# A dispatch kernel's weights as long rows dealt out by TensorE, and a third load cut in two with the stores held behind it

## The chip, the cores and the metric

The kernel runs on one core of one Trainium2 chip. The metric is device time in microseconds (us) of one execution; times given are medians of several runs. A core has five engines that run their own instruction streams (TensorE = PE, VectorE = DVE, ScalarE = ACT, GpSimd = POOL, SyncE = SP) and 16 DMA engines that move data between the main memory and the on-chip buffer of 128 partitions. In this program DMAs are issued from two queues: SyncE's, which the profile calls q1, and ScalarE's, which it calls q10.

## What is computed

Each token's row of 512 numbers is written out twice, each time multiplied by a weight of its own. `x` is 16 x 1024 tokens of 512 floats (33.5 MB), the weights are two floats a token, the output is 67 MB.

```python
def reference(x, expert_indices, expert_weights):
    k = expert_indices.shape[-1]              # 2
    x_expanded = x[:, :, np.newaxis, :].repeat(k, axis=2)
    weights = expert_weights[..., np.newaxis]
    return (x_expanded * weights).astype(np.float32)
```

The indices are not used beyond their shape.

## The kernel before

The 16,384 tokens are cut in five tiles of 25 tokens per partition and a last one of 3 (`groups`, `LAST`, L32 to L34): partition p of a tile holds 25 tokens that follow each other in memory, so that a load has 128 rows of 51,200 bytes. Two buffers hold x (`x_pool`, L44), a small one the last three tokens (`z_tile`), and a single buffer `o_ring` (L48) holds the output of one tile, 25 x 1024 floats per partition. Each tile's output is made and stored in two halves, tokens 0 to 12 and 13 to 24 (`emit`, L137), and the halves of the next tile go to the same places, so a half can only be filled again when its store has landed.

`fill` (L131) divides a half between two engines: VectorE takes the first 8 tokens (9 in the first tile) in `tensor_tensor` instructions of up to four tokens (L116), ScalarE the others in one `mul` for each token and weight (L106). Both read the weights from `w_tile`, where partition p holds the two weights of each of its tokens.

The order of the work is the program's order on each engine. ScalarE issues the loads of x: first 9 tokens of the first tile, then its other 16 (`FIRST`, L35), then the second tile (L79). The third tile's load goes out when the first tile's products are done (L147), with a small copy into `z_tile` ahead of it (L76) that makes the z load wait, and the z load behind it (L87). The fourth and fifth loads follow the second and third tiles. SyncE first issues six loads of weights (L93): for each tile 128 rows of 200 bytes, for the last three tokens 128 rows of 24 bytes. Behind them on the same queue stand all stores (L141), each of which waits for the products of its half.

Of the kernel before, what the change touches and what calls it, by code (L numbers as in the profile page):

```python
# [1 line left out]

# [4 lines left out]


@with_exitstack
def kernel(  # L10
    ctx: ExitStack,
    tc: tile.TileContext,
    x: bass.AP,
    expert_indices: bass.AP,
    expert_weights: bass.AP,
    out: bass.AP,
):
    nc = tc.nc

    batch, seq, hidden = x.shape  # L20
    k = expert_weights.shape[-1]
    P = nc.NUM_PARTITIONS
    ntok = batch * seq
    assert ntok % P == 0
    A_TOTAL = ntok // P

    f32 = mybir.dt.float32
    row = k * hidden
    CH = 4


    groups = [25, 25, 25, 25, 25]  # L32
    TX = max(groups)
    LAST = 3  # L34
    FIRST = [9, 16]  # L35
    SHARES = [[9, 9], [8, 8]]
    assert sum(groups) + LAST == A_TOTAL

    xf = x.rearrange("b s h -> (b s) h")
    of = out.rearrange("b s k h -> (b s) (k h)")  # L40
    wf = expert_weights.rearrange("b s k -> (b s) k")

    w_pool = ctx.enter_context(tc.tile_pool(name="w_pool", bufs=1))
    x_pool = ctx.enter_context(tc.tile_pool(name="x_pool", bufs=2))  # L44
    o_pool = ctx.enter_context(tc.tile_pool(name="o_pool", bufs=1))

    w_tile = w_pool.tile([P, A_TOTAL * k], f32)
    o_ring = o_pool.tile([P, TX * row], f32)  # L48

    def rows(of_all, done, T):  # L50
        return of_all[done * P : (done + T) * P, :].rearrange(
            "(p a) n -> p (a n)", a=T
        )


    if LAST:
        z_pool = ctx.enter_context(tc.tile_pool(name="z_pool", bufs=1))
        z_tile = z_pool.tile([P, LAST * hidden], f32)

    tiles = []  # L60
    done = 0
    for n in groups:
        tiles.append((done, n))
        done += n

    loaded = []

    def load(i):
        if i >= len(tiles):
            return  # L70
        done, n = tiles[i]
        x_tile = x_pool.tile([P, TX * hidden], f32)
        src = rows(xf, done, n)
        steps = FIRST if i == 0 else [n]
        if i == 2 and LAST:
            nc.scalar.copy(out=z_tile[:, :1], in_=o_ring[:, TX * row - 1 :])  # L76
        for e, step in enumerate(steps):
            at = sum(steps[:e])
            nc.scalar.dma_start(  # L79
                out=x_tile[:, at * hidden : (at + step) * hidden],  # L80
                in_=src[:, at * hidden : (at + step) * hidden],
            )
            if i == 0 and e == 0:
                for g in range(len(tiles) + 1):
                    weights(g)
        if i == 2 and LAST:
            nc.scalar.dma_start(out=z_tile, in_=rows(xf, A_TOTAL - LAST, LAST))  # L87
        loaded.append(x_tile)


    def weights(e):
        at, n = tiles[e] if e < len(tiles) else (A_TOTAL - LAST, LAST)
        nc.sync.dma_start(  # L93
            out=w_tile[:, at * k : (at + n) * k], in_=rows(wf, at, n)
        )

    def product(engine, o_tile, t, x_in, c, m):

        o = t * row
        if engine is not None:  # L100
            for e in range(m * k):
                out_e = o_tile[:, o + e * hidden : o + (e + 1) * hidden]
                in_e = x_in[:, e // k * hidden : (e // k + 1) * hidden]
                w_e = w_tile[:, c + e : c + e + 1]
                if engine is nc.scalar or engine is nc.any and (c + e) % 3 == 2:
                    nc.scalar.mul(out=out_e, in_=in_e, mul=w_e)  # L106
                else:
                    nc.vector.tensor_scalar(
                        out=out_e,
                        in0=in_e,  # L110
                        scalar1=w_e,
                        scalar2=None,
                        op0=mybir.AluOpType.mult,
                    )
            return
        nc.vector.tensor_tensor(  # L116
            out=o_tile[:, o : o + m * row].rearrange(
                "p (t k h) -> p t k h", t=m, k=k
            ),
            in0=x_in[:, : m * hidden]  # L120
            .rearrange("p (t h) -> p t h", t=m)
            .unsqueeze(2)
            .to_broadcast([P, m, k, hidden]),
            in1=w_tile[:, c : c + m * k]
            .rearrange("p (t k) -> p t k", t=m)
            .unsqueeze(3)
            .to_broadcast([P, m, k, hidden]),
            op=mybir.AluOpType.mult,
        )

    def fill(o_tile, x_in, c, m, v):  # L131
        for t in range(0, v, CH):
            u = min(t + CH, v)
            product(None, o_tile, t, x_in[:, t * hidden : u * hidden], c + t * k, u - t)
        product(nc.scalar, o_tile, v, x_in[:, v * hidden :], c + v * k, m - v)

    def emit(src, dst, c, cuts, shares):  # L137
        for at, to, v in zip(cuts, cuts[1:], shares):
            o_tile = o_ring[:, at * row : to * row]
            fill(o_tile, src[:, at * hidden : to * hidden], c + at * k, to - at, v)  # L140
            nc.sync.dma_start(out=dst[:, at * row : to * row], in_=o_tile)  # L141

    for i in range(2):
        load(i)
    for i, (done, n) in enumerate(tiles):
        emit(loaded[i], rows(of, done, n), done * k, [0, 13, n], SHARES[min(i, 1)])
        load(i + 2)  # L147
    emit(
        z_tile,
        rows(of, A_TOTAL - LAST, LAST),  # L150
        (A_TOTAL - LAST) * k,
        [0, LAST],
        [LAST],
    )

# [1 line left out]
_INS = ['x', 'expert_indices', 'expert_weights']  # L157
_OUTS = [((16, 1024, 2, 512), 'float32')]


# [23 lines left out]
```

## Time and profile before

| | |
|---|---|
| median of 3 runs | 239.5 us (239.43 to 239.72) |
| the profiled execution's own time | 239.73 us |
| its span, first to last instruction | 238.0 us |
| VectorE, ScalarE, GpSimd busy | 93.2, 55.2, 0.2 us |
| read from and written to main memory | 33.69 and 67.11 MB |
| mean rate over the span | 424 GB/s |

The page cuts the span in 40 slices of about 6 us; a digit is the busy share of a slice in tenths. The line of the DMA engines gives the mean of all 16. The queue lines give packets, megabytes and the time that the packets took as a share of 16 engines over the window asked for. A packet is one row of a transfer, or the small write that reports its end. In lists of instructions the columns are start, duration, engine, line and tiles (or, in groups, busy time and mean of one in ns, then idle time before).

### The profile page before, as it was taken

The page shows a single profiled execution, that of the slowest core. Times are in us where ns is not written, and L with a number is a line of the kernel's source. Part 1 is how long each engine was busy: PE and PEld are TensorE (multiplying, and loading weights), DVE is VectorE, ACT ScalarE, POOL GpSimd, SP SyncE. Part 2 cuts the span into 40 slices and gives each one's busy share as a digit, 9 for nine tenths or more (in the row PEclk, how much of TensorE's full clock was granted, in tenths as well). Part 3 has the DMA queues.
Part 4 walks back from the last instruction along what each step waited for, and adds up shares of the span by engine and source line. Part 5 has one row for each costly group of instructions (what it writes and reads, how often), then busy time and mean ns, then how long its engine had stood idle before and what let it go on. Part 6 is the DMA issues. An engine that isn't in the chain of part 4 may idle for free.

```text
span 238.0 us, 214 instructions
## 1 busy us (share of the span) xinstructions
DVE 93.2 (39%) x23; ACT 55.2 (23%) x88; POOL 0.2 (0%) x4
## 2 busy tenths in 40 slices
DVE  0599800000059193086005902920085292861300
ACT  0008800000054170081005302700080280800000
POOL 0000000000000000000000000000000000000000
DMA  6999999999999999999999999999999999999996
GB/s 252 445 415 493 475 415 414 415 386 457 430 406 397 434 439 456 458 430 415 405 435 484 430 434 434 413 405 431 490 430 448 417 397 423 457 448 438 438 397 264
DMA packets 3457, 100.80 MB, mean 424 GB/s; under 512 B 1152, under 2 KB 1152, under 8 KB 1280
## 3 DMA queue, kind: packets, MB, share of 16 engines
q1 hardware_dynamic: 2448, 67.24, 65.5%
q10 hardware_dynamic: 1008, 33.55, 33.1%
q14 instruction: 1, 0.01, 0.0%
HBM read 33.69 MB, written 67.11 MB: 424 GB/s over the span
## 4 chain that ended last, share of the span: by engine, by line
DMA 69%; DVE 16%; issue 5%; ACT 3%; ACTq 0%; DVEq 0%; SPq 0%
DMA out_dram<-o_ring 62%; DVE o_ring L116 16%; DMA x_tile<-in_x_dram 7%; ACT o_ring L106 2%; ACT L106 1%; ACTq L79 0%; DVEq L116 0%; SPq L141 0%; ACTq L106 0%
## 5 line engine op out<-in xcount | busy, mean ns | idle before, releaser
L116 DVE TENSOR_TENSOR o_ring<-x_tile,w_tile 128x4096 f32<-128x4096 f32 (+1 forms) x22 | 89.8, 4130 | 122.4 <-DMA out_dram<-o_ring 102.8
L106 ACT ACTIVATE o_ring<-x_tile,w_tile 128x512 f32<-128x512 f32 x86 | 53.7, 708 | 134.4 <-DMA out_dram<-o_ring 134.4
L116 DVE TENSOR_TENSOR o_ring<-z_tile,w_tile 128x3072 f32<-128x3072 f32 x1 | 3.4, 3359 | 7.0 <-DMA out_dram<-o_ring 7.0
L106 ACT ACT_TABLE_LOAD x1 | 1.3, 1283 | 18.8 <-DMA x_tile<-in_x_dram 18.8
L76 ACT COPY z_tile<-o_ring 128x1 f32<-128x1 f32 x1 | 0.2, 191 | 0.0
L168 POOL MEMSET const-bfloat16-1.0<- 128x1 bf16 x1 | 0.1, 102 | 0.0
L168 POOL MEMSET const-uint8-127<- 128x1 uint8 x1 | 0.1, 102 | 0.0
L168 POOL MEMSET const-float32-1.0<- 128x1 f32 x1 | 0.1, 99 | 0.0
L168 POOL MEMSET const-float32-0.0<- 128x1 f32 x1 | 0.1, 98 | 0.2 <-issue 0.2
## 6 DMA issues: line engine op xcount, KB each, us to landing
out_dram<-o_ring SPq DMA_DIRECT2D x5, 6656.0 KB, 32.7
out_dram<-o_ring SPq DMA_DIRECT2D x5, 6144.0 KB, 36.4
x_tile<-in_x_dram ACTq DMA_DIRECT2D x4, 6400.0 KB, 29.7
x_tile<-in_x_dram ACTq DMA_DIRECT2D x1, 4096.0 KB, 17.6
x_tile<-in_x_dram ACTq DMA_DIRECT2D x1, 2304.0 KB, 8.1
out_dram<-o_ring SPq DMA_DIRECT2D x1, 1536.0 KB, 14.6
z_tile<-in_x_dram ACTq DMA_DIRECT2D x1, 768.0 KB, 10.5
w_tile<-in_expert_weights_dram SPq DMA_DIRECT2D x5, 25.0 KB, 24.7
```

What stands on the lines that cost most here:

```text
L76: nc.scalar.copy(out=z_tile[:, :1], in_=o_ring[:, TX * row - 1 :])
L106: nc.scalar.mul(out=out_e, in_=in_e, mul=w_e)
L116: nc.vector.tensor_tensor(out=o_tile[:, o : o + m * row].rearrange("p (t k h) -> p t k h", t=m, k=k), in0=x_in[:, : m * hidden] .rearrange ...
L168: nc = _bacc.Bacc("TRN2", target_bir_lowering=False, num_devices=1)
```

## The change

Two things are changed.

Weights. For each of the five tiles the weights come as 16 rows of 1600 bytes (8 partitions' worth in each) in four DMAs, to the tail of `o_ring`, which is not yet in use. There, `deal` brings them to their 128 partitions: a VectorE copy puts the rows in line, eight TensorE transposes for each part turn 16 rows at a time, a VectorE copy puts them in order, a transpose turns them back, and a VectorE copy writes `w_tile`. The parts are tile 0, tiles 1 and 2, and tiles 3 and 4. The transposes need an identity matrix, which GpSimd makes with a memset and an `affine_select`. The last three tokens' weights come as before.

Loads and stores. The third tile is loaded as 21 and 4 tokens. The first tile's two stores are no longer issued behind their halves, but after a chain of three small GpSimd copies: the first reads two values that the 21-token load has brought, the second reads one value of each half of `o_ring`, the third writes these back, so that the stores, which read them, have to wait for it.

The order on the engines of the built program: on VectorE the lining copies of all three parts, two ordered copies, the first part's dealt weights and the third ordered copy stand ahead of the first product, and the other two parts' dealt weights between the first three products. On GpSimd a library reload stands between the memset and the select. On ScalarE the load of 21 tokens stands ahead of the small copy into `z_tile`, the loads of 4 tokens and of z behind it; the 21 tokens wait for ScalarE's fourteen products and for five of VectorE's six.

```diff
-    FIRST = [9, 16]
-    SHARES = [[9, 9], [8, 8]]
+    STEPS = {0: [9, 16], 2: [21, 4]}
...
+    parts = [(0, 1), (1, 3), (3, G)]
+    room = o_ring[:, TX * row - 2 * G * Q * c - len(parts) * P - P :]
...
+    def weights(g, to):
+        nc.sync.dma_start(
+            out=room[:R, g * Q * c : to * Q * c].rearrange(
+                "r (g m) -> r g m", g=to - g
+            ),
+            in_=wf[g * TX * P : to * TX * P, :].rearrange(
+                "(g r m) n -> r g (m n)", g=to - g, r=R
+            ),
+        )
+
+    def deal():
+        nc.gpsimd.memset(eye, 1.0)
+        nc.gpsimd.affine_select(
+            out=eye,
+            in_=eye,
+            pattern=[[-1, P]],
+            compare_op=mybir.AluOpType.is_equal,
+            fill=0.0,
+            base=0,
+            channel_multiplier=1,
+        )
+        back = ps_pool.tile([P, G * c], f32)
+        for e, (g, to) in enumerate(parts):
+            m = (to - g) * c
+            mid = ps_pool.tile([m, P], f32, name=f"mid{e}")
+            flat = turned[:m, e * P : (e + 1) * P]
+            near = lined[:, g * Q * c : to * Q * c].rearrange("r (q m) -> r q m", q=Q)
+            nc.vector.tensor_copy(
+                out=near.rearrange("r q (g n) -> r g q n", g=to - g),
+                in_=raw[:, g:to],
+            )
+            for q in range(Q):
+                nc.tensor.transpose(
+                    mid[:, q * R : (q + 1) * R], near[:, q, :], eye[:R, :R]
+                )
+            nc.vector.tensor_copy(
+                out=flat.rearrange("p (r q) -> p q r", q=Q),
+                in_=mid.rearrange("p (q r) -> p q r", q=Q),
+            )
+            nc.tensor.transpose(back[:, g * c : to * c], flat, eye[:m, :m])
+            nc.vector.tensor_copy(
+                out=w_tile[:, g * c : to * c], in_=back[:, g * c : to * c]
+            )
...
+    load(0, 0)
+    weights(0, 1)
+    weights(1, 3)
+    weights(3, 4)
+    weights(4, 5)
...
+    deal()
+    load(0, 1)
+    load(1, 0)
     for i, (done, n) in enumerate(tiles):
...
+        for at, to in halves:
+            make(x_pair[i % 2], done * k, at, to, 9 if i == 0 else 8)
+            if i > 0:
+                store(dst, at, to)
+        if i == 0:
+            nc.scalar.copy(out=z_tile[:, :1], in_=o_ring[:, TX * row - 1 :])
+            load(2, 0)
+            load(2, 1)
+            nc.scalar.dma_start(out=z_tile, in_=rows(xf, A_TOTAL - LAST, LAST))
+
+            nc.gpsimd.tensor_copy(out=hold, in_=x_pair[0][:, :2])
+            held = o_ring[:, : 13 * row + 1 : 13 * row]
+            nc.gpsimd.tensor_copy(out=hold, in_=held)
+            nc.gpsimd.tensor_copy(out=held, in_=hold)
+            for at, to in halves:
+                store(dst, at, to)
+        elif i + 2 < G:
+            load(i + 2, 0)
```

More of the change, by code (lines that the diff above doesn't have):

```diff
@@ L53, in rows @@
         )
-    if LAST:
-        z_pool = ctx.enter_context(tc.tile_pool(name="z_pool", bufs=1))
-        z_tile = z_pool.tile([P, LAST * hidden], f32)
     tiles = []
@@ L64 @@
         done += n
[L66 to L81, printed above, removed]
-            )
[L83 to L88, printed above, removed]
@@ L91, in weights, with load @@
[L91 to L95, printed above, removed]
+    def load(i, e):
+        at = sum(STEPS.get(i, groups[i : i + 1])[:e])
+        to = at + STEPS.get(i, groups[i : i + 1])[e]
+        part = slice(at * hidden, to * hidden)
+        nc.scalar.dma_start(out=x_pair[i % 2][:, part], in_=rows(xf, *tiles[i])[:, part])
+    G = len(groups)
+    R = 16
@@ L135, in fill, with make, store @@
         product(nc.scalar, o_tile, v, x_in[:, v * hidden :], c + v * k, m - v)
[L137 to L144, printed above, removed]
-    for i, (done, n) in enumerate(tiles):
[L146 to L154, printed above, removed]
+    def make(src, c, at, to, v):
+        o_tile = o_ring[:, at * row : to * row]
+        fill(o_tile, src[:, at * hidden : to * hidden], c + at * k, to - at, v)
+    def store(dst, at, to):
+        nc.sync.dma_start(
+            out=dst[:, at * row : to * row], in_=o_ring[:, at * row : to * row]
+        )
+    load(0, 0)
[3 more added lines that the diff above has]
+    weights(4, 5)
+    nc.sync.dma_start(
+        out=w_tile[:, G * c :], in_=rows(wf, A_TOTAL - LAST, LAST)
+    )
+    deal()
+    load(0, 1)
+    load(1, 0)
+    for i, (done, n) in enumerate(tiles):
+        dst = rows(of, done, n)
+        halves = [(0, 13), (13, n)]
+        for at, to in halves:
[15 more added lines that the diff above has]
+            load(i + 2, 0)
+    make(z_tile, (A_TOTAL - LAST) * k, 0, LAST, LAST)
+    store(rows(of, A_TOTAL - LAST, LAST), 0, LAST)
 _INS = ['x', 'expert_indices', 'expert_weights']
```

14 lines of the change are left out of this document (13 added, 1 removed).

## The prediction, made before the change was run

> **What bounds the kernel now.** I read the page first: the busy shares, the packet line and the queues.
>
> ```profile
> span 238.0 us, 214 instructions
> DVE 93.2 (39%) x23; ACT 55.2 (23%) x88; POOL 0.2 (0%) x4
> DMA  6999999999999999999999999999999999999996
> DMA packets 3457, 100.80 MB, mean 424 GB/s; under 512 B 1152, under 2 KB 1152, under 8 KB 1280
> ...
> q1 hardware_dynamic: 2448, 67.24, 65.5%
> q10 hardware_dynamic: 1008, 33.55, 33.1%
> ```
>
> No compute engine is busy for even half of the span, while the DMA engines stand at nine tenths in every slice but the first and the last. The two queues, q1 (SyncE: weights and stores) and q10 (ScalarE: loads of x), together take 98.6% of 16 engines over the span. So the span is the time in which 16 DMA engines move 100.8 MB, and only three things can change it: cheaper packets, DMA engines that stall on a packet, or a moment in which both queues are empty.
>
> Next come the queue lines of three windows: 5 to 45 us (loads with weight rows among them), 47 to 53 us (the three-token z tile, the last weights, the first stores) and 55 to 90 us (stores alone).
>
> ```profile
> q10 hardware_dynamic: 481, 17.68, 102.3%
> q1 hardware_dynamic: 481, 0.08, 1.1%
> ```
> ```profile
> q10 hardware_dynamic: 160, 0.79, 42.2%
> q1 hardware_dynamic: 259, 1.03, 41.9%
> ```
> ```profile
> q1 hardware_dynamic: 333, 15.50, 102.3%
> ```
>
> A packet is counted in the window where it begins, so a share may pass 100%; bytes over packet time give the rate all the same. Stores: 15.50 MB in 1.023 x 35 us is 433 GB/s. Loads: 17.68 MB in 1.023 x 40 us is 432 GB/s. The z tile: 0.79 MB in 0.422 x 6 us = 2.53 us of all engines, where 433 GB/s would need 1.82 us; **0.71 us is lost** there. Weight rows: 481 in 0.011 x 640 engine-us, that is 14.6 ns each. They are cheap, but they come one by one between the long x rows, which the landing times show:
>
> ```profile
> out_dram<-o_ring SPq DMA_DIRECT2D x5, 6656.0 KB, 32.7
> ...
> w_tile<-in_expert_weights_dram SPq DMA_DIRECT2D x5, 25.0 KB, 24.7
> ```
> ```profile
> DMA to landing us min/median/max: 5.3/32.1/49.0
> ```
>
> The second line is of the six weight DMAs alone: the first 25 KB take 5.3 us, the slowest DMA 49 us. The first store stands behind them on its queue, as the chain of waits has it:
>
> ```profile
> 25.12 42.86 DMA out_dram<-o_ring
> ```
>
> It lands at 67.98 us, and its 6.82 MB need 15.7 us at 433 GB/s, so it began at about 52 us, though it was issued at 25.12. No byte is lost by that, because q10 is full until then.
>
> **The change part by part.**
>
> (a) *Weights as long rows.* Out go 5 x 128 rows of 200 bytes; the 128 rows of 24 bytes stay. At 14.6 ns, 640 rows are 9.3 engine-us, over 16 engines 0.58 us. In come 80 rows of 1600 bytes. At 433/16 = 27.1 bytes per ns a row is 59 ns, and 200 bytes in 14.6 ns leave 7 ns beside the 7.4 for bytes, so 66 ns, five to an engine: 0.33 us. **Gain 0.25 us**; were the rows' fixed part nothing or twice as much, 0.28 to 0.21.
>
> (b) *The z tile moves beside stores.* Its rows were slow while they ran with only tiny rows on the other queue. After the change the stores are released when the 21 tokens have landed, and z's 6 KB rows alternate with 52 KB store rows. Where loads and stores alternate now, nothing is lost: the window from 95 to 99 us, in which the fourth tile's load sets in between stores, has
>
> ```profile
> DMA packets 38, 1.77 MB, mean 442 GB/s; under 512 B 4, under 2 KB 4, under 8 KB 4
> ```
>
> So between nothing and 0.71 us comes back. I take 0.65, near that row. The four tokens (8 KB rows, 1.05 MB, 2.42 us at 433 GB/s) now run alone before z. If they stalled as z did (2.53/1.82 = 1.39) they would lose 0.94 us. They lie 50 KB apart like the long rows and have no weight rows among them, so I take nothing; the 0.94 stays for the range. Splitting adds 8 packets of 7 ns to each engine: 0.06 us. **Gain 0.59 us.**
>
> (c) *The deal, and what waits for it.* New on the path of the first tile: GpSimd makes an identity, VectorE copies, TensorE transposes 27 times, VectorE copies back, and only then come the products. Who waits is seen in the timeline and the forms:
>
> ```profile
> 0.73 3.11 SPq L93 DMA_DIRECT2D w_tile<-in_expert_weights_dram  x6
> 0.73 8.50 ACTq L79 DMA_DIRECT2D x_tile<-in_x_dram  x3
> 8.90 19.73 DVE L116 TENSOR_TENSOR o_ring<-x_tile,w_tile 128x4096 f32<-128x4096 f32 x6 [8.90 <-DMA x_tile<-in_x_dram]
> ...
> 20.08 8.69 ACT L106 ACTIVATE o_ring<-x_tile,w_tile 128x512 f32<-128x512 f32 x14
> 25.12 197.72 SPq L141 DMA_DIRECT2D out_dram<-o_ring  x11
> 28.80 0.19 ACT L76 COPY z_tile<-o_ring 128x1 f32<-128x1 f32 x1
> 28.86 0.35 ACTq L79 DMA_DIRECT2D x_tile<-in_x_dram  x1
> ```
> ```profile
> L116 DVE TENSOR_TENSOR o_ring<-x_tile,w_tile 128x1024 f32<-128x1024 f32 x2 | 2.4, 1216 | 0.0
> L106 ACT ACT_TABLE_LOAD x1 | 1.3, 1283 | 18.8 <-DMA x_tile<-in_x_dram 18.8
> ...
> L168 POOL MEMSET const-uint8-127<- 128x1 uint8 x1 | 0.1, 102 | 0.0
> ```
>
> VectorE works without a gap from 8.90 to 28.63 us; ScalarE ends at 28.77, and the third tile's load is issued at 28.86 into the buffer that both have read. How late may it be? The lead from an issue to its first packet is about 1 us: issued at 0.73, packets begin in the slice from 1.5 us, in the first ten microseconds cut in quarters:
>
> ```profile
> DMA  0000001995393988969919919839879399300993
> ```
>
> In front of the third load q10 holds the second tile. The sixteen tokens ahead of that land at 18.79 (ScalarE's table load waited for them), and its 6.55 MB take 15.2 us more: landed at 34.0. I take 1.2 us, an estimate near the lead, between the first engine's last row and the landing: q10 runs dry at about 32.8, and the third load must be issued by 31.8. In the built program its 21 tokens wait for VectorE's fifth product only, not the sixth of 1.2 us, and for ScalarE's fourteen. VectorE's fifth ended at 28.63 - 1.22 = 27.4, so VectorE may be 4.4 us late and ScalarE 3.0 for nothing.
>
> How late is it? The built program puts on VectorE, ahead of the first product, three lining copies, three copies of transposes and one of the dealt weights; two more stand between the products. No such copy is in the trace; per column the 1024-column product gives 1.2 ns, so 800 columns are 0.95 us and 100 to 128 columns 0.15. The last weights, issued fourth at about 2.2 us, land 5.3 us later if they do as the first did: 7.5. Then a copy (0.95), eight transposes (no row; between 0.1 us, the smallest instruction shown, and 0.7 us, an ACTIVATE, and I take 0.1: 0.8), three short copies (0.45) and handovers: the first product starts at about 10 us instead of 8.9, and two copies (0.3) come later. VectorE is 1.4 us late, under 4.4. **Cost nothing**; the queue in front of the third load hides it. At 0.7 us per transpose the 24 first ones alone would take 17 us, and the cover would be gone; from there each microsecond is one.
>
> The other input is the identity. The built program has a library reload on GpSimd between the memset and the select. Its time is in no row: the small end is 0.1 us (MEMSET), then 1.28 us (the table load of ScalarE), then 5.3 us for 25 KB that come through the same busy DMA engines at that moment, and at the far end 24.7 us. I take 5.3: ready at 0.73 + 0.1 + 5.3 + 0.2 = 6.3 us, before the last weights. [...]
>
> (d) *The hold.* SyncE's first store waits for three tiny GpSimd copies behind the 21 tokens; behind it in SyncE's order stand all other stores, and ScalarE's and VectorE's work on the second tile waits for those. The chain: landing, three copies with handovers (0.1 us each by the MEMSET row, I take 0.2), issue and lead 1.0 us: 1.7 us. Meanwhile q10 still has the four tokens and z, 2.4 + 1.8 = 4.2 us. **Cost nothing**; at 1 us a copy the chain is 4 us and still covered.
>
> From there to the end stores follow without a gap as now; the fourth and fifth loads and the last products keep their places. Head and tail (1.6 us before the first packet, about 1.2 after the last) stay.
>
> **Sum:** 0.25 + 0.59 = 0.84, and about 0.05 for completion packets and rows that no longer make turns; call it 0.9. Against the profiled execution's span: 238.0 - 0.9 = 237.1 us. That execution took 239.73 us, 0.23 over the median of 239.5; the forecast for the median is **238.6 us**.
>
> **The rivals.**
>
> *The identity or the transposes come late* (ends slower). The place is the third load's issue; the price is 1 us for each microsecond of idle queue; it decides once the first product starts after 13.0 us (8.9 + 4.4 less the two later copies), that is, the identity later than about 10 us, with 2.6 us of transposes and copies behind it, or a library load longer than 9 us. For it: a small transfer among long rows has taken far more than 9 us (24.7). Against: at the start the same 25 KB took 5.3, and 4.4 us of cover is a lot. With a library load of 12 us the first product starts at 0.73 + 0.1 + 12 + 0.2 + 2.6 = 15.6, and the queue stands empty for 2.6 us: 239.5 - 0.9 + 2.6 = 241.2 us; at 24.7 it would be 254.
>
> *Stalls only change their place.* The four tokens lose what z lost, up to 0.94 us, or z stays slow beside the stores. For it: 8 KB rows are nearer to z's 6 KB than to anything else shown. Then only (a) is left, or a little less than nothing: 239.3 us.
>
> *The hold is late.* If GpSimd needs 2 us for each copy, stores begin 2.8 us after q10 ran empty: 239.5 - 0.9 + 2.8 = 241.4. Against it: the 0.1 us MEMSET.
>
> *It doesn't do what it says*: weights already cost only 0.6 us, so all of (a) could shrink by longer row times (1600 bytes as slow as z's rows, 1.39 x 66 ns, five to an engine, give 0.46 us in place of 0.33). Then 238.7, inside the forecast.
>
> **How the numbers follow.** Forecast 0.55; identity or transposes late 0.23; stalls moved 0.12; hold late 0.06; other delays, such as one DMA engine loaded with code and so behind the rest, 0.04. A measurement of this kernel can tell about 0.2% (0.5 us) from no change. The forecast's own range is 238.2 to 239.0, faster. Stalls moved is the same time. The other three are slower but for a few cases that miss the cover by under 1 us. That gives faster 0.55, same 0.14, slower 0.31. For 8 in 10 the range goes from 238.1 (all 0.58 us of weight rows and all 0.71 of z's) to 241.6, which takes in both late cases at their prices and leaves out only their far part.
>
> **What would show it.** Weights: q1 under 2% of the engines in the first ten microseconds and about 80 + 128 small rows in place of 768. Deal: first product at about 10 us, the 21 tokens' load issued at about 29 us, and no slice under nine tenths near 33 us. Hold: the first store issued near 47 us, no dip at 46 to 50 us. Stalls: z's rows near 433 GB/s over their packet time. The prediction is wrong if the DMA row dips near 33 or 48 us, if the first product starts after 13 us, or if rows of 8 KB show more than 0.3 us each.

## The result and the profile after

The changed kernel takes **243.4 us** (median of 6 runs, 243.06 to 244.9) against 239.61 us (239.43 to 239.81) for the kernel before on the same chip: ratio 1.0167 [1.0141, 1.0193], so 1.7% slower and well beyond the noise. The forecast was 238.6 us with a range of 238.1 to 241.6; the time lies outside it. The profiled execution, the longest of the six, took 244.9 us; its span of 243.2 us is 5.2 us longer than before's, where the medians differ by 3.8. Of the runs below, one execution of e13 was disturbed (245.55 us, against 241.5 to 241.68 of its other three) and is left out of that run's time and ratio; e13's trace, with the time of its third load, is of that execution.

The page of the changed kernel, the lines that answer to those of before:

```profile
span 243.2 us, 293 instructions
PE 3.4 (1%) x27; PEld 2.5 (1%) x27; DVE 95.9 (39%) x32; ACT 55.1 (23%) x88; POOL 1.3 (1%) x9
DMA  7999989999999999999999999999999999999992
DMA packets 3025, 100.80 MB, mean 415 GB/s; under 512 B 512, under 2 KB 592, under 8 KB 720
...
q1 hardware_dynamic: 1872, 67.24, 64.0%
q10 hardware_dynamic: 1152, 33.55, 33.5%
```

The change did what it says: 80 rows of 1600 bytes stand in place of 640 of 200, and the deal adds only 2.7 us to VectorE. The same bytes take longer, at 415 in place of 424 GB/s, and the page shows no hole, but for a dip to 8 in the sixth slice. Where the time went is in the order of events. The timeline of the changed kernel, its first 51 us (start, duration, engine; in brackets the idle time before and what ended it):

```profile
1.07 0.29 POOL L98 TENSOR_SCALAR_AFFINE_SELECT o_ring<-o_ring 128x128 f32<-128x128 f32 x1
3.08 0.36 DVE L113 COPY o_ring<-o_ring 16x400 f32<-16x400 f32 x1 [3.08 <-DMA o_ring<-in_expert_weights_dram]
...
8.44 0.56 DVE L113 COPY o_ring<-o_ring 16x800 f32<-16x800 f32 x1 [5.01 <-DMA o_ring<-in_expert_weights_dram]
...
12.19 0.56 DVE L113 COPY o_ring<-o_ring 16x800 f32<-16x800 f32 x1 [3.19 <-DMA o_ring<-in_expert_weights_dram]
...
14.32 4.41 DVE L149 TENSOR_TENSOR o_ring<-x,w_tile 128x4096 f32<-128x4096 f32 x1
...
33.28 0.33 ACTq L70 DMA_DIRECT2D x<-in_x_dram  x1
...
49.40 0.19 POOL L203 COPY hold<-x 128x2 f32<-128x2 f32 x1 [48.03 <-DMA x<-in_x_dram]
...
50.10 0.88 SPq L175 DMA_DIRECT2D out_dram<-o_ring  x2
```

The identity is ready at 1.36 us. The three lining copies wait for weights, the last until 12.19 us; so the first product starts at 14.32 us, the third load goes out at 33.28 us, its 21 tokens land at 49.40 us (the first GpSimd copy starts then) and the first store is issued at 50.10 us. The chain of waits shows what this becomes. First the changed kernel's stores in the chain (start, duration), then those of before behind its first one:

```profile
50.10 20.28 DMA out_dram<-o_ring
...
79.41 25.27 DMA out_dram<-o_ring
...
113.62 27.66 DMA out_dram<-o_ring
...
160.78 33.23 DMA out_dram<-o_ring
```
```profile
76.99 24.96 DMA out_dram<-o_ring
...
110.89 25.75 DMA out_dram<-o_ring
...
156.12 32.68 DMA out_dram<-o_ring
```

Start and duration give the landings: 70.38, 104.68, 141.28 and 194.01 us after, 67.98, 101.95, 136.64 and 188.80 before (the first from the chain row in the prediction). The kernel is 2.4 us late when the first of these stores has landed, 2.7 at the second, 4.6 at the third, 5.2 at the fourth. **About half of the loss of this execution is there when that store lands, at 70 us; most of the rest arises between 105 and 141 us.**

Part of the second half shows in the rows of the loads between 98 and 105 us, where the fourth load sets in (q10: packets, MB, share of 16 engines); the changed kernel first, then the one before:

```profile
q10 hardware_dynamic: 31, 1.59, 72.9%
```
```profile
q10 hardware_dynamic: 38, 1.95, 64.2%
```

1.59 MB in 0.729 x 7 us are 312 GB/s, before 434: 1.4 us of packet time that moves nothing. (The same kernel's second trace, e1, has only 0.3 us of it; see there.) And the end is frayed: the share of the DMA engines in the last slices of 2 us, after, then before.

```profile
236.00:238.00 2.00, 0.00 (x0) 0.00 (x0) 0.00 (x0) 0.00 (x0) 0.00 (x0) 1.00 0.98 418
238.00:240.00 2.00, 0.00 (x0) 0.00 (x0) 0.00 (x0) 0.00 (x0) 0.00 (x0) 1.00 0.32 135
240.00:242.00 2.00, 0.00 (x0) 0.00 (x0) 0.00 (x0) 0.00 (x0) 0.00 (x0) 1.00 0.09 37
```
```profile
236.00:238.00 2.00, 0.00 (x0) 0.00 (x0) 0.00 (x0) 1.00 0.08 31
```

After, some engines work on for more than 2 us while most are done (0.32 and 0.09); before, all stop within a microsecond (0.08 of 2 us). The packets of the trace say it more exactly. Of the 16 small writes that report the end of the last store, the last ones of the kernel, all end between 236.0 and 236.8 us before; after, 14 end between 238.3 and 239.5 us and two at 241.1 and 242.0. The kernel ends with its slowest engine.

### The profile page after: what moved, and what is told of

Same layout as the page of the kernel before. It is cut to its first block, busy times and chain, and to the rows that moved or that the text cites. A ratio compares the mean times of both kernels' runs of the same rounds, so it can differ in the third digit from the quotient of the medians.

```text
span 243.2 us, 293 instructions
## 1 busy us (share of the span) xinstructions
PE 3.4 (1%) x27; PEld 2.5 (1%) x27; DVE 95.9 (39%) x32; ACT 55.1 (23%) x88; POOL 1.3 (1%) x9
## 4 chain that ended last, share of the span: by engine, by line
DMA 53%; issue 24%; DVE 16%; POOL 0%; POOLq 0%; DVEq 0%; SPq 0%
DMA out_dram<-o_ring 53%; DVE o_ring L149 16%; POOL o_ring L98 0%; DVEq L149 0%; POOLq L237 0%; POOL o_ring L97 0%; POOL hold L203 0%; POOL hold L205 0%; SPq L175 0%; POOLq L205 0%; POOLq L226 0%
## 5 line engine op out<-in xcount | busy, mean ns | idle before, releaser
L149 DVE TENSOR_TENSOR o_ring<-x,w_tile 128x4096 f32<-128x4096 f32 (+1 forms) x22 | 89.9, 4128 | 112.9 <-DMA out_dram<-o_ring 102.2
L139 ACT ACTIVATE o_ring<-x,w_tile 128x512 f32<-128x512 f32 x86 | 53.7, 708 | 134.8 <-DMA out_dram<-o_ring 134.8
L113 DVE COPY o_ring<-o_ring 16x800 f32<-16x800 f32 (+1 forms) x3 | 1.5, 495 | 11.3 <-DMA o_ring<-in_expert_weights_dram 11.3
L118 PE MATMUL mid<-o_ring 16*100 16x16 f32 (+1 forms) x24 | 2.4, 230 | 11.4 <-DVE o_ring L113 11.4
L118 PEld LDWEIGHTS mid<-o_ring 16*100 16x100 f32 (+1 forms) x24 | 2.0, 169 | 11.7 <-DVE o_ring L113 8.1
L125 PE MATMUL back<-o_ring 100*128 100x100 f32 (+1 forms) x3 | 1.2, 401 | 4.5 <-DVE w_tile L126 4.5
L121 DVE COPY o_ring<-mid 100x128 f32<-100x128 f32 (+1 forms) x3 | 1.0, 387 | 0.2 <-PE mid L118 0.2
L126 DVE COPY w_tile<-back 128x100 f32<-128x100 f32 (+1 forms) x3 | 0.7, 236 | 0.3 <-PE back L125 0.3
L125 PEld LDWEIGHTS back<-o_ring 100*128 100x128 f32 (+1 forms) x3 | 0.5, 182 | 4.9 <-DVE w_tile L126 4.8
```

Of the source, the lines that this page charges most:

```text
L113: nc.vector.tensor_copy(out=near.rearrange("r q (g n) -> r g q n", g=to - g), in_=raw[:, g:to],)
L118: nc.tensor.transpose(mid[:, q * R : (q + 1) * R], near[:, q, :], eye[:R, :R])
L121: nc.vector.tensor_copy(out=flat.rearrange("p (r q) -> p q r", q=Q), in_=mid.rearrange("p (q r) -> p q r", q=Q),)
L125: nc.tensor.transpose(back[:, g * c : to * c], flat, eye[:m, :m])
L126: nc.vector.tensor_copy(out=w_tile[:, g * c : to * c], in_=back[:, g * c : to * c])
L149: nc.vector.tensor_tensor(out=o_tile[:, o : o + m * row].rearrange("p (t k h) -> p t k h", t=m, k=k), in0=x_in[:, : m * hidden] .rearrange ...
```

## The experiments

Four explanations stood against each other. **Late load:** the third load comes too late to follow the second without a gap, and the hold has taken away the stores that would fill it. **Hold:** holding the stores costs by itself. **Weights:** the long rows and the deal cost by themselves. **Shifted buffers:** the hold's flag tile of 8 bytes a partition, kept in 32, moves x, z and `o_ring` in the built program from 128 to 160 modulo 256 bytes. Ratios are to the kernel before on the same chip (239.62 to 239.72 us). Where a recorded expectation says "table", it means `z_tile`.

| run | what it is | us, median | ratio |
|---|---|---|---|
| e1_again | changed kernel once more | 244.5 | 1.0197 [1.017, 1.0224] |
| e2_weights_alone | long rows and deal, no hold, third tile in one | 239.63 | 0.9999 [0.999, 1.0009] |
| e3_hold_alone | 21 + 4 and hold, short weight rows | 240.94 | 1.0047 [1.0031, 1.0063] |
| e4_deal_later | changed, tiles 1 to 4 dealt later | 241.96 | 1.0105 [1.0074, 1.0137] |
| e5_no_hold | changed, without the hold | 239.64 | 1.0003 [0.9992, 1.0014] |
| e6_more_cover | changed, z loaded ahead of the third tile, that in 18 + 7 | 241.1 | 1.0057 [1.0043, 1.0072] |
| e7_z_later | before, z behind the fourth load | 239.65 | 1.0001 [0.9992, 1.001] |
| e8_aligned | changed, flag tile of 256 bytes | 242.87 | 1.0142 [1.0122, 1.0161] |
| e9_hold_aligned | e3, flag tile of 256 bytes | 240.5 | 1.003 [1.0019, 1.0041] |
| e10_cover_aligned | e6, flag tile of 256 bytes | 240.59 | 1.0038 [1.0026, 1.005] |
| e11_no_hold_shifted | e5 with an 8-byte tile | 239.89 | 1.0014 [0.9998, 1.0029] |
| e12_hold_late | e9, products 2 x 1.22 us later | 240.46 | 1.0037 [1.0023, 1.0051] |
| e13_hold_later | e9, 3 x 1.22 us later | 241.6 | 1.0079 [1.0062, 1.0096] |
| e14_late_no_hold | before, 2 x 1.22 us later | 239.95 | 1.0011 [1.0, 1.0022] |
| e15_hold_latest | e9, 5 x 1.22 us later | 242.94 | 1.015 [1.0123, 1.0178] |
| e16_latest_no_hold | before, 5 x 1.22 us later | 239.73 | 1.0007 [0.9997, 1.0016] |
| e17_rows_adjacent | before, with 16 long rows a tile besides, into adjacent partitions | 244.95 (one execution) | none |
| e18_rows_spread | e17, the rows into every eighth partition | 243.89 (one execution) | none |

### Each half alone

> The changed kernel once more, unedited, to see which of its losses come back. In the first profile the packet times beyond those of before sum to (per engine): 1.1 us up to 10 us (loads beside the weight rows), 1.0 us at 32 to 36 us (queue dry, the third load issued at 33.28), 1.4 us at 98 to 105 us (fourth load's first rows up to 4.1 us), and the slowest engine ends 2.5 us further behind the middle one than before. Theory A (late first product): the first two and the spread come back, the 1.4 us at 98 us does not, span 241.3 to 242.0. Rival B (the handover of loads and stores makes all of it): the 1.4 us at the fourth load comes back too, span about 243.

The loss is there again: 244.5 us, and its trace has a span of 242.4 us, between the two that were expected. The first four stores of its chain land 2.4, 1.9, 3.8 and 4.4 us later than before's, so here too 1.9 us arise between the second and the third. But from 98 to 105 us q10 moves 2.20 MB in 0.774 x 7 us, 406 GB/s: 0.3 us lost, not 1.4. So the slow rows at 98 us aren't what makes that part each time; what does is not shown.

> The weights part alone: 16 rows a tile and the deal, but the third tile loaded in one step and the first tile's stores issued behind their halves, as before. Theory A (long weight rows and the late first product): 241 to 243 us, the third load issued after 33 us; but the stores may fill the dry moment near 34 us, since nothing holds them, which would bring it down to 240 to 241. Rival B (hold and split are to blame): 239.3 to 239.9.

```diff
-    STEPS = {0: [9, 16], 2: [21, 4]}
+    STEPS = {0: [9, 16]}
...
-            if i > 0:
-                store(dst, at, to)
+            store(dst, at, to)
...
```

The three GpSimd copies and the flag tile go too, and the third tile is loaded in one. 239.63 us: the weights' half neither gains nor loses, though its first product starts at 14.25 us.

> The other part alone: third tile as 21 and 4 tokens and the hold, weights as 128 rows of 200 bytes straight to their place. Theory A: first product at 8.9 us, third load issued at 28.9, no dry queue; the stores stand behind the weight rows until about 50 us as before, so 239.3 to 240.0 us. Rival B: the engines spread at 47 to 55 us and the time is 241 to 243 us.

```diff
-    weights(0, 1)
...
+    for e in range(G):
+        nc.sync.dma_start(
+            out=w_tile[:, e * c : (e + 1) * c], in_=rows(wf, *tiles[e])
+        )
...
-    deal()
...
```

240.94 us, between the two that were expected: the hold's half costs 1.3 us, though the third load goes out at 27.70 us. The halves add up to 1.3 us and the whole costs 3.8: they act on each other.

> The changed kernel with the deal of tiles 1 to 4 moved behind the first half's products on VectorE (a tiny copy that reads the third product's output makes it wait), so that the first product waits for the first tile's weights alone. Theory A: first product at about 10 us (x lands then), third load issued before 32 us, no dry queue at 32 to 36 us; gain 1.0 us of dry time and most of the 2.5 us of spread: 240 to 241.5 us. Rival B: no gain, 243 to 244 us, though the queue is no longer dry.

```diff
...
+            if i == 0 and at == 0:
+                turn(list(enumerate(parts))[1:])
...
```

Here `turn` is the part of `deal` behind the identity, called for the first tile's part ahead of the loop and for the others at this place. The first product moved up to 10.50 us, but the deal of the other tiles then held up the second half, and the third load was still issued at 32.98 us, only 0.3 us earlier. 241.96 us, with a wide interval; as a test of the late load it is inconclusive.

> The changed kernel without the hold: the first tile's stores are issued behind their halves again; the weights' rows, the deal and the 21 and 4 tokens stay. Theory A2 (the deal makes the third load late, and only the hold, which leaves both queues without work, turns that into lost time and into engines out of step): the third load is issued after 33 us as in the changed kernel, but the stores run, no idle time at 32 to 37 us, 239.4 to 239.9 us. Rival B2 (the step of 21 and 4 tokens is at fault): 241 us or more.

```diff
-            if i > 0:
-                store(dst, at, to)
+            store(dst, at, to)
...
-            nc.gpsimd.tensor_copy(out=hold, in_=x_pair[0][:, :2])
-            held = o_ring[:, : 13 * row + 1 : 13 * row]
-            nc.gpsimd.tensor_copy(out=hold, in_=held)
-            nc.gpsimd.tensor_copy(out=held, in_=hold)
```

The queue rows of its timeline (SyncE's stores, ScalarE's third load):

```profile
26.22 8.45 SPq L174 DMA_DIRECT2D out_dram<-o_ring  x2
33.21 0.34 ACTq L69 DMA_DIRECT2D x<-in_x_dram  x1
```

The third load is as late as in the changed kernel (33.21 and 33.28 us), but stores stand in the queue from 26.22 us, and it takes 239.64 us. The late load alone costs nothing.

> The changed kernel with more in the load queue ahead of the third tile: the last three tokens are loaded right behind the second tile (1.9 us of work), and the third tile is cut 18 and 7 so that the hold has the same cover as before (7 tokens in place of 4 and the z tile). First product and third load stay as late as they are. Theory A2: no idle time at 32 to 37 us and the first rows of the third load not slow, which gives back 1.0 us and the part of the spread that came from there: 241 to 242.5 us; the slower rows beside the weights (1.1 us) and the slow first rows of the fourth and fifth load stay. Rival (the hold itself costs, however the load comes): 243 to 244.5 us.

```diff
-    STEPS = {0: [9, 16], 2: [21, 4]}
+    STEPS = {0: [9, 16], 2: [18, 7]}
...
     load(1, 0)
+    nc.scalar.dma_start(out=z_tile, in_=rows(xf, A_TOTAL - LAST, LAST))
...
```

Weights, deal and hold are all there, but 1.8 us of z rows stand in the queue where it went dry. 241.1 us: the loss shrinks from 3.8 to 1.4 us, about what the hold costs alone.

> The kernel before with one edit: the last three tokens are loaded with the fourth tile, beside stores, in place of behind the third tile, beside weight rows. If the 0.65 us that z's rows lose at 47 to 51 us is due to their standing alone among small rows, they run at full rate there and the time is 238.8 to 239.1 us (239.6 before). Rival (the engines fall out of step when the stores start earlier): 239.6 to 240.5 us.

```diff
-        if i == 2 and LAST:
+        if i == 3 and LAST:
```

239.65 us: moving z off its bad place gains nothing. From 45 to 50 us this kernel's q10 has

```profile
q10 hardware_dynamic: 32, 0.82, 55.5%
```

0.82 MB in 0.555 x 5 us are 295 GB/s, where 433 GB/s would need 0.9 us less. These are the third tile's last rows, where z used to follow. The stall was not z's; it fell on other rows.

### The address of the buffers

> The changed kernel with the flag tile of the hold padded to 256 bytes a partition, so that the token tiles, the table tile and the result ring start at the same byte offset (128 modulo 256) as in the kernel before; hold, deal and the load in 21 and 4 tokens stay. Theory A (the queue that runs dry at 32 to 37 us, because the third load comes at 33.3 us and no stores cover it): the time stays at 243 to 244.5 us, the fourth load's rows at 98 to 105 us stay slow. Theory B (the 32 bytes by which the flag tile moved these buffers make row packets slow): 239.7 to 241 us, the gap at 32 to 37 us still there, the rows at 98 to 105 us no longer slow, the ends of the 16 engines within 1 us.

```diff
-    hold = w_pool.tile([P, 2], f32)
+    hold_tile = w_pool.tile([P, 64], f32)
+    hold = hold_tile[:, :2]
```

> The hold and the load in 21 and 4 alone, weights as 200-byte rows as before, the flag tile padded to 256 bytes. Theory A: 240.9 us as in the same kernel with the 8-byte tile (240.2 to 241.5), since the hold sets its time. Theory B: 239.0 to 239.7 us, as the hold costs nothing where the third load is issued at 27.7 us.

> Table loaded behind the second tile, third tile as 18 and 7 tokens, hold and deal kept, the flag tile padded to 256 bytes. Theory A: 241.1 us as with the 8-byte tile. Theory B: 238.5 to 239.7 us: no dry queue and no shifted buffers.

> The changed kernel without the hold (stores behind each half), with an 8-byte tile that nothing waits for and that shifts token tiles, table and result ring by 32 bytes. Theory A: 239.6 us, as without the tile. Theory B: 240.5 to 242 us, with slow rows where the buffers are used again.

The padded kernels come out at 242.87, 240.5 and 240.59 us, the unpadded ones at 243.4 to 244.5, 240.94 and 241.1; without a hold the shift makes 239.89 of 239.64. All four pairs have the same sign and 0.25 to 1.6 us between them, but the intervals of most pairs overlap: the shift may cost some 0.4 us, and it is not the main cause; e8 remains 3.2 us slower than before. No run takes the shift further apart.

### Lateness without weight rows

> The hold and the load in 21 and 4 with the weights as 200-byte rows and the padded flag tile (240.5 us), and two additional products of one token on VectorE ahead of the first half (2.75 us each, their results are overwritten), so that the third load is issued at 33.1 us in place of 27.6. Theory A (the lateness of the third load with no stores to cover it): 242 to 243.5 us, the queue with gaps or slow rows at 32 to 37 us. Rival C (the weight rows and the deal are what costs): 240.5 us, as without the delay.

```diff
     load(1, 0)
+    for _ in range(2):
+        product(None, o_ring, 0, x_pair[0], 0, 1)
```

> As e12 with three additional products: third load at 35.9 us. Theory A: by about the 2.75 us of one product longer than e12, 245 to 246 us, with 1.5 to 2.5 us of idle transfer engines at 32 to 37 us. Rival C: 240.5 us.

> The kernel before with the same two additional products ahead of its first half: third load near 34.4 us, stores behind each half. Theory A: 239.6 us, since the stores of the first half cover the queue. A theory by which a late third load costs in any case: 241 us or more.

An extra product took 1.22 us, not 2.75, so the third load came at 29.96 us (e12) and 31.32 us (e13), short of the 33.1 and 35.9 that were meant. At 29.96 nothing changed; at 31.32 the kernel took 1.1 us more. Without the hold the two products move the load to 31.02 us (e14), and the time is 239.95 us, at most 0.5 us more than before's by its interval. The next two settle it.

> As e12 with five additional products of 1.22 us: third load at 33.7 us, as late as in the changed kernel, weights as 200-byte rows. Theory A (lateness without stores to cover it): 242.5 to 244 us, idle and slow rows of together 0.7 us or more at 32 to 37 us. Rival C (weight rows and deal): at most 241.6 us, as at 31.3 us.

> The kernel before with the same five additional products, stores behind each half: third load near 34.5 us. Theory A: 239.6 to 240 us, no idle at 32 to 37 us, since the first half's stores feed the queue. A theory by which a late third load costs in any case: 242 us or more.

The third load, the landing of its 21 tokens and the first store in the chain, e9 first, then e15 with five extra products:

```profile
27.58 0.33 ACTq L68 DMA_DIRECT2D x<-in_x_dram  x1
...
46.98 0.18 POOL L149 COPY hold_tile<-x 128x2 f32<-128x2 f32 x1 [46.55 <-DMA x<-in_x_dram]
```
```profile
47.69 19.37 DMA out_dram<-o_ring
```
```profile
33.54 0.33 ACTq L68 DMA_DIRECT2D x<-in_x_dram  x1
...
49.12 0.18 POOL L151 COPY hold_tile<-x 128x2 f32<-128x2 f32 x1 [48.68 <-DMA x<-in_x_dram]
```
```profile
49.82 19.79 DMA out_dram<-o_ring
```

The load is issued 5.96 us later, its tokens land 2.14 us later, the first store lands 2.55 us later (69.61 for 67.06), and the kernel takes 242.94 (242.39 to 243.81) in place of 240.5 us: 2.4 us, without one long weight row. So much of the lateness as the queue ahead did not cover is paid at about one to one. Between 30 and 36 us q10 has, in e9 and in e15:

```profile
q10 hardware_dynamic: 64, 2.20, 84.7%
```
```profile
q10 hardware_dynamic: 48, 1.51, 69.5%
```

16 rows fewer, and 362 in place of 433 GB/s over their packet time: a gap, and slow first rows behind it. Counted from the starts and lengths of all packets in the traces, the 16 engines stand idle from 32 to 36 us for 1.2 us each, on the mean, in e15, for 0.4 us in the changed kernel, and not at all in e9, e5 and e16. The same five products without the hold (e16):

```profile
25.14 9.96 SPq L141 DMA_DIRECT2D out_dram<-o_ring  x2
34.72 0.35 ACTq L79 DMA_DIRECT2D x_tile<-in_x_dram  x1
```

The third load is later still, 34.72 us, and it takes 239.73 us. **The late load costs only where the hold keeps the stores out of the gap**; the weights explanation falls.

### The rows beside the long weight rows

> The kernel before with four more transfers behind its weight loads: the weights once more as 16 rows of 1600 bytes a tile into partitions 0 to 15 of an unused part of the result ring; nobody reads them. If the long rows slow the token rows beside them, the packet time beyond the nominal one up to 10 us rises from 0.4 us to 1.4 us a transfer engine; if the deal's own work is the reason, it stays at 0.4.

> As e17, but the 16 rows end in every eighth partition. If it is the adjacent partitions that slow the token rows, the packet time beyond the nominal one up to 10 us is back at 0.4 to 0.6 us; if it is the long rows as such, it is 1.4 us as in e17.

```diff
+    def extra():
+        room = o_ring[:, TX * row - 2000 :]
+        for g, to in [(0, 1), (1, 3), (3, 4), (4, 5)]:
+            nc.sync.dma_start(
+                out=room[:16, g * 400 : to * 400].rearrange(
...
```

The edit puts the extra rows ahead of the weight loads, not behind them as the expectation has it. e18 has `room[::8, ...]` there. q10 from 2 to 10 us in the changed kernel, in before, in e17 and in e18:

```profile
q10 hardware_dynamic: 156, 2.81, 96.1%
```
```profile
q10 hardware_dynamic: 172, 3.33, 99.0%
```
```profile
q10 hardware_dynamic: 139, 2.27, 75.4%
```
```profile
q10 hardware_dynamic: 136, 2.21, 67.5%
```

Over their packet time the token rows run at 365, 420, 376 and 409 GB/s. Beside 16 long rows a tile into adjacent partitions they were slow (365 and 376), beside the same rows spread over the partitions much less so (409). But each is one execution, both kernels moved fewer token rows in these 8 us than before (2.2 for 3.3 MB), and both took longer as a whole (244.95 and 243.89 us against 239.62), with the short weight rows queued behind the extra ones. For the time of the kernel they decide nothing.

## Why the prediction was wrong

*What bounds the kernel* held: no compute engine rose above 39%, and rows that stall and a moment with both queues empty, two of its three things, are what is seen to cost time. Engines that end at different times were not on its list.

*(a), gain 0.25 us.* The packets are there as predicted, and by themselves they gain about that: counted in the traces, the 640 short rows take 0.71 us an engine before, the 80 long ones 0.47 after. But the step left out their neighbours. From 2 to 10 us the token rows beside them take 0.961 x 8 = 7.69 us for 2.81 MB, 1.2 us more than at 433 GB/s; before it was 0.2. That 1 us is more than the gain. In e2, z's rows go beside stores and run at 420 GB/s over their packet time, so their loss is back as well, and still e2 has no gain to show.

*(b), gain 0.59 us.* Locally right: z's rows and the four tokens, from 47.3 to 54.6 us,

```profile
q10 hardware_dynamic: 305, 1.88, 62.8%
```

move 1.88 MB in 4.58 us, 410 GB/s; 0.24 us are lost in place of 0.71. But e7 frees z of its stall and gains nothing, as the rival "stalls only change their place" had it for other rows.

*(c), "Cost nothing; the queue in front of the third load hides it": this step failed.* Its threshold was a little late: the third load was to be issued by 31.8 us; in e12 29.96 us is free, in e13 31.32 us costs 1.1 us. What failed above all is the lateness. The last weights were put at 7.5 us, by the landing time of the first DMA, though the row beside it showed 24.7 us for the median; they came at 12.19. The transposes were no problem:

```profile
L118 PE MATMUL mid<-o_ring 16*100 16x16 f32 (+1 forms) x24 | 2.4, 230 | 11.4 <-DVE o_ring L113 11.4
```

24 of them are 2.4 us of busy time. The first product started at 14.32 us, 5.4 us late where 4.4 were allowed, beyond the 13.0 us that the rival had named as its deciding point.

*(d), "Cost nothing": this step failed too.* Its chain of three copies is as short as estimated, 0.70 us from the landing to the store's issue (49.40 to 50.10). What it missed is that the stores it holds were the cover of (c): with them in the queue a load at 33.2 or 34.7 us costs nothing (e5, e16). The two steps were priced one by one, each against the kernel before, where the other's cover was still there. Besides, the hold costs 0.8 us (e9) even with an early load.

The rival "identity or transposes late" had the right place, a dry queue ahead of the third load. Its price was too low: 1.3 us beyond the 13.0, by its own sum, is 239.5 - 0.9 + 1.3 = 239.9 us, and 243.4 was measured. The 0.9 did not come, the hold took 0.8, and the late load under the hold 2.4. Its cause was wrong too. The identity was ready at 1.36 us; its select began 0.07 us after the memset ended (1.00 to 1.07), and the first transposes used it at 3.58: the library reload that was put at 5.3 us is not to be seen in this trace, and the select itself took 0.29 us.

Added up from the runs: weights 0.0 (e2), hold 0.8 (e9), late load under the hold 2.4 (e15 less e9), shifted buffers some 0.4: 3.6 of the 3.8 us. The kernel that has all of these but the shift, e8, bears the sum out: 0.8 and 2.4 make 3.2, and it is 3.2 us slower. Three things stay open. Why does the hold cost 0.8 us by itself? Its first store even lands earlier than before's (67.06 against 67.98), and the loss arises later. Why do two engines end so late in the changed kernel, and what makes its 1.9 us between 105 and 141 us? In e15, with a longer gap, the last writes end within 1.3 us of each other and that stretch adds 0.1 us; so neither belongs to the gap alone. And what is the stall of 0.7 to 1.1 us that falls on z's rows before, on the third tile's in e7, on the second tile's last rows in e16 (0.82 MB in 2.99 us from 30 to 36 us), and on rows beside the weights in e2 (2.79 MB in 7.51 us from 2 to 10 us), at one and the same time of 239.6 us? Of all versions tried, none is faster than the kernel before.

## What to carry to other kernels

Where transfers bound a kernel, price a change that delays a load together with any change that holds other transfers back: here a late load was free while something else stood in the queues (34.72 us, 239.73 us in e16), and cost about its whole uncovered lateness when nothing did (landing 2.14 us later, 2.4 us in e15). For small transfers among large ones take the spread of landing times at that place, not the first one's (here 5.3 us for the first, 24.7 for the median and 49.0 for the slowest in the kernel before). A test with the stall moved (e7) tells at the price of one run whether a stall belongs to the rows it was seen on.

## What the runs showed of the hardware

Where the queue ran dry for part of 30 to 36 us, the loss was more than the gap (1.2 us of idle engines and 2.4 us of time in e15), and the rows around it were slow (362 GB/s in e15, 390 in the changed kernel with 2.33 MB in 5.97 us, against 433 in e9). Beside sixteen rows of 1600 bytes a tile into adjacent partitions long rows ran at 365 to 376 GB/s in place of 420, and beside the same rows into every eighth partition at 409 (one execution). Three small GpSimd copies in a row passed a landing on to another queue in 0.70 us.
